# A hybrid attention and gating block on one core: POOL's elementwise work of the first part on ACT and DVE, a second load of x for its norm, and output weights loaded as whole tiles

## The chip, the cores and the metric

The kernel runs on one core of a Trainium2 chip. The metric is device time in microseconds (us) of one execution, lower is better. The engines are named as the profile names them: PE (TensorE, matmuls), DVE (VectorE), ACT (ScalarE), POOL (GpSimd) and SP (SyncE), whose queue issues nearly all DMAs here.

## The reference, cut to what matters

One layer for 1024 tokens of width 1024, all in float32. Eight q heads and two kv heads of 64 columns attend over all tokens; a second branch gates u with a position mix of v_in in chunks of 128 tokens; both are merged and projected.

```
h = rmsnorm(x, norm_gain)
z = h @ w_in                                   # 1024 x 4864
q, k, v, gate_a, u_in, v_in, gate_b, g_merge = split(z)
q, k = axial_rope(rmsnorm(q, q_gain)), axial_rope(rmsnorm(k, k_gain))
attn = softmax(q k^T / 8) v * silu(gate_a);            y_a = attn @ w_proj_attn
vv = layernorm(gelu(v_in)); v_mix = w_spatial . vv + b_spatial
gm = gelu(u_in) * v_mix * silu(gate_b);                y_b = gm @ w_proj_gmlp
g = sigmoid(g_merge + b_merge)
out = rmsnorm(x + (g0 * y_a + g1 * y_b) @ w_out, final_gain)
```

## The kernel before

**High and low parts.** Most products are made of three matmuls: an operand is split into a rounded part and the difference (`xh` and `xl` for x, `wh` and `wl`, `nh` and `nl`, `woh` and `wol` for weights), and `mm3` (lines 174 to 177) takes high by high, high by low and low by high into one PSUM bank. `split` (lines 115 to 117) makes the high part on an engine that the caller names (`hi_part`, lines 107 to 113: POOL with a multiplication, ACT with a copy) and the low part as a difference, on DVE unless named otherwise.

**First part.** x comes transposed (`xT`) in eight tiles `xraw0` to `xraw7` of 128 columns by 1024 tokens, each 512 KB, through four buffers with the tag `T16` (`load_x`, lines 147 to 164): ACT makes `xh` with the norm's gain, DVE makes `xl`. Behind each tile PE adds its share of k and v for all tokens, 24 matmuls `kv` of 256 columns (lines 181 to 199). Weights come as `wraw` tiles of 256 KB through four buffers; here POOL makes their high parts. The root of the norm needs the sum of squares over the columns of x, which lie across partitions here: `add_square` (lines 166 to 172) squares each `xraw` on ACT and adds it into `xsq`, on POOL for five tiles and on DVE for two; eight small matmuls `ssx` with ones (line 236; 16 in the profile's count) then sum over partitions. DVE and POOL make `rstd` of that (`power_rstd`, lines 131 to 133).

**v_in, k, q.** `nat_weights` (lines 210 to 221) loads eight half tiles for v_in, later for q, high parts on POOL (`NWE`), low parts on DVE (`nl`). `v_group` (lines 364 to 371) makes 48 matmuls `v` for 256 tokens, and ACT takes them out of PSUM times `rstdh` (`vst`). `v_finish` makes gelu and layer norm, and the spatial matmuls `sp`. The spatial weights are loaded as `wspr`, split with the high part on POOL, and `wsum` sums them by a matmul (lines 256 to 275). The rotary tables (line 395), v's two scalings (lines 407 and 428) and half of each rotation (line 330: `ktmp`, `qtmp`) are multiplied on POOL.

**Attention.** 64 half steps (`scores`, line 549 on: 4 matmuls `s`, DVE's maximum, ACT's exponential, normalising on ACT and DVE, a transposing DMA `T<-p`) and 32 `mix` steps (matmuls `o`), with the matmuls of gates and u (`ga`, `gb`, `u`) between them as filling.

**Merge and output.** Steps written out in `MORDER` (line 739): `w` loads a pair's gate weights, `g` makes the pair's gates by seven products (`g`, `g7T`, with weights `wg`, `wg7T` that ACT and DVE split), `A` makes the forms of the gated attention branch (in buffers with the tags `xh`, `kT` and `xl`), `a` projects it by seven products (`y`, `y03T`, with weights `wp`, `wp03T`), and `o` calls `out_weights` (lines 845 to 852): 16 loads of 256 KB through the four `wraw` buffers, high parts on ACT, low parts on DVE, and splits the first two of the eight tiles of y. Behind the loop the other six tiles of y are split (line 923), and 384 matmuls `out` follow (lines 938 to 948). x is loaded once more, as `xr`, for the residual.

**What sets the order.** The program is written as one stream; a scheduler puts each engine's instructions in order by a simulated time line, and buffers are waited for by semaphores. Each engine, and SP's queue of DMA issues, then works strictly along its own line.

Of the kernel before, what the change touches and what calls it, by code (L numbers as in the profile page):

```python
# [30 lines left out]
def hybrid_block_kernel(  # L31
# [134 lines left out]
    def add_square(dt, raw):  # L166
        if dt == 0:
            act.activation(xsq, raw, AF.Square)
        else:
# [1 line left out]
            act.activation(sq, raw, AF.Square)
            XSQ[dt].tensor_tensor(out=xsq, in0=xsq, in1=sq, op=ALU.add)
# [62 lines left out]
    for tt in range(NT):  # L235
        pe.matmul(ssp[:, 2 * tt:2 * tt + 2], xsq[:, C(tt)], ones[:, 0:2], start=True, stop=True)
# [84 lines left out]
    def rope(src, tmp, A, B, n, nh):  # L321
        for k in range(n if nh > 2 else nh):
# [6 lines left out]
            for b in range(2):  # L329
                pool.tensor_tensor(out=t5[:, :, :, b, :], in0=s5[:, :, :, 1 - b, :],  # L330
                                   in1=b5[:, :, :, b, :].broadcast_to([P, 8, 2, 16]), op=ALU.mult)
# [96 lines left out]
    pool.tensor_tensor(out=v3, in0=v3, in1=vinv[:, None, :].broadcast_to([P, 8, 128]), op=ALU.mult)  # L428
# [591 lines left out]
```

## Time and profile before

| | |
|---|---|
| median of 3 runs | 770.64 us (766.96 to 770.91) |
| profiled execution, whole | 771.03 us |
| its span | 769.3 us |
| PE, DVE, ACT, POOL busy | 725.2, 612.9, 434.7, 160.1 us |
| mean granted clock of PE | 0.979 |
| HBM read, written | 42.88 MB, 4.19 MB |

Busy times are unions of an engine's instructions; PE's are pipelined, so that 94% busy is not 94% of its peak. Idle time is given with the instruction that ended it. `L117` is line 117 above; a helper's line stands for all its callers, so tiles tell the place. Names on the left of an arrow are written, those on the right read.

### The profile page before, as it was taken

What the parts mean: (1) busy time and instruction counts of PE and PEld (TensorE: products, weight loads), DVE (VectorE), ACT (ScalarE), POOL (GpSimd) and SP (SyncE); (2) the same over time, 40 slices, a digit from 0 to 9 for tenths busy, and PEclk for the clock granted to TensorE, in tenths of its full rate; (3) what the DMA queues carried; (4) which work ended last, traced back from release to release, by engine and by line L of the source; (5) the groups of instructions that cost most, each with busy time, mean ns of one, the idle gap of its engine ahead of it and who ended that gap; (6) DMA issues with size and microseconds to landing.
All of it is one profiled execution on the core that took longest, in us unless ns stands there. A gap on an engine that the chain in (4) does not pass through costs nothing.

```text
span 769.3 us, 9864 instructions
## 1 busy us (share of the span) xinstructions
PE 725.2 (94%) x3577; PEld 535.9 (70%) x3577; DVE 612.9 (80%) x915; ACT 434.7 (57%) x752; POOL 160.1 (21%) x131
## 2 busy tenths in 40 slices
PE   7989999998999899999999997899999998799996
PEld 7868888776888677788777884355464645388884
DVE  6965897699888989988889999999888898833223
ACT  7304457386878877878777478555474535521101
POOL 4930665345123221123200000010000000000000
PEclk9979999998999999999999999999999999999998
DMA  7321120135668779869899930130030204520211
GB/s 279 106 82 35 29 82 16 40 58 109 135 137 149 145 146 163 176 133 172 165 192 267 250 84 1 55 120 19 20 117 1 71 27 152 170 102 29 82 55 55
DMA packets 152609, 81.27 MB, mean 106 GB/s; under 512 B 135408, under 2 KB 136048, under 8 KB 152560
## 3 DMA queue, kind: packets, MB, share of 16 engines
q1 hardware_dynamic: 152272, 80.36, 42.5%
q8 instruction: 28, 0.46, 0.2%
q10 hardware_dynamic: 288, 0.28, 0.1%
q14 instruction: 21, 0.17, 0.1%
HBM read 42.88 MB, written 4.19 MB: 61 GB/s over the span
## 4 chain that ended last, share of the span: by engine, by line
PE 53%; DVE 21%; DMA 11%; ACT 6%; issue 6%; POOL 2%; SPq 1%; POOLq 0%; DVEq 0%; ACTq 0%
DMA T<-p 8%; PE out L175 4%; PE out L177 4%; PE out L176 4%; PE o L579 3%; DVE p L568 3%; DVE nm L557 2%; PE g L175 2%; PE g L176 2%; PE g L177 2%; DMA wraw<-in_wall_dram 2%; PE v L176 1%; PE v L177 1%; PE s L554 1%; PE v L175 1%
## 5 line engine op out<-in xcount | busy, mean ns | idle before, releaser
L568 DVE SCALAR_TENSOR_TENSOR p<-P,ri,p 128x1024 f16<-128x1024 f32 x64 | 85.8, 1343 | 22.2 <-ACT p L567 21.8
L567 ACT ACTIVATE p<-P,ri 128x1024 f16<-128x1024 f32 x64 | 73.1, 1143 | 25.1 <-DMA T<-p 17.4
L561 ACT ACTIVATE P<-s,nm 128x1024 f32<-128x1024 f32 x64 | 71.3, 1114 | 24.1 <-DVE nm L557 15.6
L557 DVE TENSOR_REDUCE nm<-s 128x1 f32<-128x1024 f32 x64 | 77.7, 1215 | 1.8 <-PE s L555 1.4
L579 PE MATMUL o<-T,vS 128*128 128x256 f16 x512 | 63.5, 278 | 4.9 <-ACT qT L355 2.9
L579 PEld LDWEIGHTS <-vS 128*128 128x128 f16 x512 | 48.2, 99 | 19.8 <-issue 8.0
L117 POOL TENSOR_TENSOR wl<-wraw,wh 128x512 fp32r<-128x512 f32 x24 | 38.8, 1620 | 101.3 <-ACT wh L111 57.4
L554 PE MATMUL s<-kT,qT 128*128 128x512 f32 x128 | 53.5, 418 | 4.0 <-ACT P L561 4.0
L677 POOL TENSOR_TENSOR scg<-scg,mhalf 128x1 f32<-128x1 f32 x8 | 7.0, 870 | 217.2 <-DVE scg L676 217.2
L555 PE MATMUL s<-kT,qT 128*128 128x512 f32 x128 | 50.5, 395 | 0.0
L950 DVE TENSOR_TENSOR xr<-out,xr 128x1024 f32<-128x1024 f32 x7 | 8.6, 1224 | 46.4 <-PE out L177 46.2
L898 ACT ACTIVATE sq<-xr 128x1024 f32<-128x1024 f32 x7 | 7.4, 1060 | 64.1 <-DVE xr L950 64.1
L175 PE MATMUL out<-woh,yhl 128*128 128x512 f32 x96 | 38.0, 396 | 0.0
L177 PE MATMUL out<-woh,yhl 128*128 128x512 f32 x96 | 37.6, 392 | 0.0
L176 PE MATMUL out<-wol,yhl 128*128 128x512 f32 x96 | 37.6, 391 | 0.0
L554 PEld LDWEIGHTS s<-kT,qT 128*128 128x128 f32 x128 | 24.1, 188 | 11.0 <-ACT P L561 6.4
L900 POOL TENSOR_TENSOR rs<-rs,mhalf 128x1 f32<-128x1 f32 x7 | 3.8, 549 | 125.5 <-DVE rs L899 125.5
L555 PEld LDWEIGHTS s<-kT,qT 128*128 128x128 f32 x128 | 24.1, 189 | 4.6 <-issue 0.2
L492 PE MATMUL ga<-xh,wh 128*128 128x512 f32 x64 | 26.1, 408 | 1.2 <-DVE ga30w L498 1.1
L175 PE MATMUL v<-nh,xh 128*128 128x512 f32 x64 | 26.8, 419 | 0.0
L492 PE MATMUL u<-xh,wh 128*128 128x512 f32 x64 | 25.6, 400 | 0.8 <-DVE uw L515 0.8
L177 PE MATMUL v<-nh,xl 128*128 128x512 f32 x64 | 26.1, 408 | 0.0
(554 smaller groups left out, 2212.9 us busy)
## 6 DMA issues: line engine op xcount, KB each, us to landing
wraw<-in_wall_dram SPq DMA_DIRECT2D x75, 256.0 KB, 3.1
graw<-in_wall_dram SPq DMA_DIRECT2D x16, 512.0 KB, 5.1
xraw<-in_xT_dram SPq DMA_DIRECT2D x15, 512.0 KB, 6.8
xr<-in_x_dram SPq DMA_DIRECT2D x8, 512.0 KB, 4.3
out_dram<-xr SPq DMA_DIRECT2D x7, 512.0 KB, 2.6
T<-p SPq DMA_TRANSPOSE x64, 4.5
wspr<-in_wsp_dram SPq DMA_DIRECT2D x2, 256.0 KB, 2.6
rtk<-in_cst_dram SPq DMA_DIRECT2D x1, 512.0 KB, 4.4
```

Source lines behind the costliest of these rows:

```text
L117: eng_lo.tensor_tensor(out=lo, in0=raw, in1=hi if hi.dtype == F16 else hi.bitcast(F32), op=ALU.subtract)
L175: pe.matmul(o, ah, bh, start=start, stop=False)
L176: pe.matmul(o, ah, bl, start=False, stop=False)
L177: pe.matmul(o, al, bh, start=False, stop=stop)
L492: pe.matmul(o, wh[:, C(dt % 4)], xh[dt][:, H(h)], start=(dt == 0), stop=False)
L554: pe.matmul(sp[:, H(hf)], qs, kT[:, 2 * v, H(hf)], start=True, stop=False)
L555: pe.matmul(sp[:, H(hf)], qs, kT[:, 2 * v + 1, H(hf)], start=False, stop=True)
L557: dve.tensor_reduce(out=nm, in_=sp, axis=AX.X, op=ALU.max, negate=True)
L561: act.activation(Pt, sp, AF.Exp, bias=nm, accum_out=rsum)
L567: act.activation(hi, Pt, AF.Copy, scale=ri)
L568: dve.scalar_tensor_tensor(out=lo, in0=Pt, scalar=ri, in1=hi, op0=ALU.mult, op1=ALU.subtract)
L579: pe.matmul(ot[:, 0:256], vS[:, kt, v, :], T[:, :, 8 * p + kt, :], start=(kt == 0 and p == 0), stop=(kt == 7 and p == 1))
```

## The change

1. High parts of kv's, v_in's, q's and the spatial weights are made on ACT, not POOL.
2. `add_square` no longer squares the transposed tiles: it loads tile `tt` of x with tokens on partitions (`xn`, 512 KB, tag `og`, two buffers), and ACT squares it in place and sums along the row into a column of `ssx`. It is called behind each of the eight v_in weights. The additions into `xsq` and those matmuls `ssx` go.
3. The rotary tables, v's two scalings and the products `ktmp` and `qtmp` are made on DVE (lines 395, 407 and 428 as line 330 in the diff). POOL keeps the powers, and in attention the low parts of filling weights and the products into `vm`.
4. `out_weights` is split: step `o` issues eight loads of 512 KB (`wor`, tag `xh`, the buffers of the gated branch's forms); `out_weight(dt)` makes the two parts of one tile by one instruction each. The first two tiles are split in step `o`, the other six behind the loop, each ahead of its tile of y. The room for the parts changes with it (`who`, `WOT`).
5. `xr` takes other buffers: three of its eight tiles stand where y's upper half stood.

```diff
-    XSQ = (dve, dve, pool, pool, pool, pool, pool, dve)
-    NWE = (pool, pool)
+    NWE = (act, act)
...
-    def add_square(dt, raw):
-        if dt == 0:
-            act.activation(xsq, raw, AF.Square)
-        else:
-            sq = t4("og", f"xsq{dt}")
-            act.activation(sq, raw, AF.Square)
-            XSQ[dt].tensor_tensor(out=xsq, in0=xsq, in1=sq, op=ALU.add)
+    def add_square(tt):
+        xn = t4("og", f"xn{tt}")
+        nc.sync.dma_start(out=xn, in_=x[C(tt), :])
+        act.activation(xn, xn, AF.Square, accum_out=ssx[:, tt:tt + 1])
...
-                split(wh[:, r], wl[:, r], wr[:, r], pool)
+                split(wh[:, r], wl[:, r], wr[:, r], act)
...
-                wh, wl = stream_w(W_KV + i // 2, i % 2)
+                wh, wl = stream_w(W_KV + i // 2, i % 2, act)
...
-    wv = nat_weights(W_VIN, range(8))
+    wv = nat_weights(W_VIN, range(8), add_square)
     ssp = ps_z("ssx")
-    for tt in range(NT):
-        pe.matmul(ssp[:, 2 * tt:2 * tt + 2], xsq[:, C(tt)], ones[:, 0:2], start=True, stop=True)
...
-        split(wsh[:, H(h)], wsl[:, H(h)], raw, pool)
+        split(wsh[:, H(h)], wsl[:, H(h)], raw, act)
...
-                pool.tensor_tensor(out=t5[:, :, :, b, :], in0=s5[:, :, :, 1 - b, :],
+                dve.tensor_tensor(out=t5[:, :, :, b, :], in0=s5[:, :, :, 1 - b, :],
...
-    def out_weights():
-        lo4 = sb.tile([P, 4, 1024], F32R, tag="kT", bufs=1, name="wol")
+    def load_out():
         for dt in range(8):
-            hi = t4("xh", f"woh{dt}", F32R)
-            lo = lo4[:, dt, :] if dt < 4 else t4("xl", f"wol{dt}", F32R)
-            for h in range(2):
-                split(hi[:, H(h)], lo[:, H(h)], load_w(W_OUT + dt, h), act, dve)
-            who.append((hi, lo))
+            raw = t4("xh", f"wor{dt}")
+            nc.sync.dma_start(out=raw, in_=wall[W_OUT + dt])
+            wor.append(raw)
+    def out_weight(dt):
...
+        act.copy(hi, wor[dt])
+        dve.tensor_tensor(out=lo, in0=wor[dt], in1=hi.bitcast(F32), op=ALU.subtract)
+        who.append((hi, lo))
...
         elif step == "o":
-            out_weights()
-            for dt in range(2):
+            load_out()
+            for dt in range(EARLY):
+                out_weight(dt)
                 split_y(dt)
...
-    for dt in range(2, 8):
+    for dt in range(EARLY, 8):
+        out_weight(dt)
         split_y(dt)
```

**SP's queue in the first part.** Before, from the fifth x tile on (`wraw00` and so on are half tiles of v_in's weights, `bsp` a constant):

```order
L153 DMA xraw4_241<-in_xT_dram 128x1024
L121 DMA wraw00_395<-in_wall_dram 128x512
L265 DMA bsp_470<-in_cst_dram 128x512
L153 DMA xraw5_280<-in_xT_dram 128x1024
L121 DMA wraw01_401<-in_wall_dram 128x512
L153 DMA xraw6_313<-in_xT_dram 128x1024
L153 DMA xraw7_352<-in_xT_dram 128x1024
L121 DMA wraw10_405<-in_wall_dram 128x512
```

After the change, from the same place:

```order
L150 DMA xraw4_231<-in_xT_dram 128x1024
L120 DMA wraw00_373<-in_wall_dram 128x512
L168 DMA xn0_379<-in_x_dram 128x1024
L168 DMA xn1_386<-in_x_dram 128x1024
L261 DMA bsp_464<-in_cst_dram 128x512
L150 DMA xraw5_267<-in_xT_dram 128x1024
L150 DMA xraw6_297<-in_xT_dram 128x1024
L120 DMA wraw01_382<-in_wall_dram 128x512
L150 DMA xraw7_333<-in_xT_dram 128x1024
L120 DMA wraw10_389<-in_wall_dram 128x512
```

Two loads of x by rows stand ahead of the sixth transposed tile now; the other six stand further down, behind the weights of v_in.

**ACT's line in the first part.** Before, from the third x tile on (`xsq2` is the square of that tile):

```order
L159 ACTIVATE xh2_170<-xraw2_169,cs_65 128x1024
L171 ACTIVATE xsq2_205<-xraw2_169 128x1024
L159 ACTIVATE xh3_209<-xraw3_208,cs_65 128x1024
L171 ACTIVATE xsq3_238<-xraw3_208 128x1024
L159 ACTIVATE xh4_242<-xraw4_241,cs_65 128x1024
L171 ACTIVATE xsq4_277<-xraw4_241 128x1024
L159 ACTIVATE xh5_281<-xraw5_280,cs_65 128x1024
```

After (`wh` and `nh` are high parts of kv's and v_in's weights):

```order
L156 ACTIVATE xh2_166<-xraw2_165,cs_65 128x1024
L110 CAST wh81_173<-wraw81_171 128x512
L156 ACTIVATE xh3_202<-xraw3_201,cs_65 128x1024
L110 CAST wh90_239<-wraw90_237 128x512
L110 CAST wh91_305<-wraw91_303 128x512
L156 ACTIVATE xh4_232<-xraw4_231,cs_65 128x1024
L110 CAST nh00_375<-wraw00_373 128x512
L169 ACTIVATE xn0_379,ssx_86<-xn0_379 128x1024
L169 ACTIVATE xn1_386,ssx_86<-xn1_386 128x1024
L156 ACTIVATE xh5_268<-xraw5_267,cs_65 128x1024
```

The squares of the transposed tiles are gone from between the `xh`; casts of weights stand there, and the first two squares by rows.

**ACT's line ahead of the last pair's gates.** Before, from the last weights of the last attention projection (`wp03T4`) to the first late weights of the last pair (`wg7T3`; `p1g7` takes its first product out of PSUM):

```order
L111 CAST wp0322_6047<-ps03_5985 128x256
L111 CAST wp03T4_6058<-wraw450_5983 128x256
L111 CAST woh1_6082<-wraw471_6087 128x512
L111 CAST woh2_6091<-wraw480_6092 128x512
L111 CAST woh2_6091<-wraw481_6096 128x512
L111 CAST woh3_6100<-wraw490_6101 128x512
L111 CAST woh3_6100<-wraw491_6105 128x512
L111 CAST woh4_6109<-wraw500_6111 128x512
L111 CAST woh4_6109<-wraw501_6115 128x512
L704 COPY p1g7_6157<-g711_6161 128x512
L684 ACTIVATE wg7T3_6210<-graw7_5955,scg7_5969 128x512
```

After:

```order
L110 CAST wp0322_6041<-ps03_5979 128x256
L858 CAST who_6082<-wor0_6066 128x1024
L858 CAST who_6082<-wor1_6068 128x1024
L110 CAST wp03T4_6052<-wraw450_5977 128x256
L858 CAST wo30_6229<-wor3_6072 128x1024
L858 CAST wo40_6236<-wor4_6074 128x1024
L700 COPY p1g7_6095<-g711_6099 128x512
L680 ACTIVATE wg7T3_6148<-graw7_5949,scg7_5963 128x512
```

Three casts of half tiles of output weights stood ahead of these rows before. Now two whole ones stand ahead of `wp03T4` and two behind it.

More of the change, by code (lines that the diff above doesn't have):

```diff
@@ L207, in hybrid_block_kernel, with nat_weights @@
         dve.tensor_copy(vn[:, r].rearrange("p (t e) -> p t e", e=128), src[:, :, 128:256])
-    def nat_weights(first, dts):
+    def nat_weights(first, dts, between=None):
         ws = []
@@ L220, in nat_weights @@
             ws.append((hi[:, H(dt % 2)], l))
+            if between is not None:
+                between(dt)
         return ws
@@ L246, in hybrid_block_kernel @@
     rstd = const([P, NT], "rstd")
-    power_rstd(rstd, ssp[:, 0:16].rearrange("p (t k) -> p t k", k=2)[:, :, 0], NT, 1.0 / D)
+    power_rstd(rstd, ssx, NT, 1.0 / D)
     bmh = const([P, 16], "bmh")
@@ L406, in hybrid_block_kernel @@
     v3 = vn.rearrange("p (t e) -> p t e", e=128)
-    pool.tensor_tensor(out=v3, in0=v3, in1=rstd[:, :, None].broadcast_to([P, 8, 128]), op=ALU.mult)
+    dve.tensor_tensor(out=v3, in0=v3, in1=rstd[:, :, None].broadcast_to([P, 8, 128]), op=ALU.mult)
     vscr = t2("vscr")
@@ L427, in hybrid_block_kernel @@
     dve.tensor_scalar(out=vsc, in0=vsc, scalar1=1.0 / (PSCALE * VSCALE), scalar2=None, op0=ALU.mult)
[L428 removed]
+    dve.tensor_tensor(out=v3, in0=v3, in1=vinv[:, None, :].broadcast_to([P, 8, 128]), op=ALU.mult)
     v4 = vn.rearrange("p (t h d) -> p t h d", h=2, d=64)
@@ L843, in hybrid_block_kernel @@
     yhl, who = {}, []
-    def out_weights():
-        lo4 = sb.tile([P, 4, 1024], F32R, tag="kT", bufs=1, name="wol")
+    wor, who4 = [], []
+    def load_out():
         for dt in range(8):
-            hi = t4("xh", f"woh{dt}", F32R)
-            lo = lo4[:, dt, :] if dt < 4 else t4("xl", f"wol{dt}", F32R)
-            for h in range(2):
-                split(hi[:, H(h)], lo[:, H(h)], load_w(W_OUT + dt, h), act, dve)
-            who.append((hi, lo))
+            raw = t4("xh", f"wor{dt}")
+            nc.sync.dma_start(out=raw, in_=wall[W_OUT + dt])
+            wor.append(raw)
+    def out_weight(dt):
+        if dt == 0:
+            who4.append(sb.tile([P, 4, 1024], F32R, tag="kT", bufs=1, name="who"))
+        if dt < 2:
+            hi, lo = who4[0][:, 2 * dt, :], who4[0][:, 2 * dt + 1, :]
+        else:
+            hi, lo = (t4(t, f"wo{dt}{k}", F32R) for k, t in enumerate(WOT[dt - 2].split()))
+        act.copy(hi, wor[dt])
+        dve.tensor_tensor(out=lo, in0=wor[dt], in1=hi.bitcast(F32), op=ALU.subtract)
+        who.append((hi, lo))
+    WOT = ("xl xl", "xh xh", "xh xh", "og og", "xh xh", "xh vS")
     def split_y(dt):
@@ L921, in finish_last @@
         nc.sync.dma_start(out=out[C(tt), H(1)], in_=y[:, H(1)])
-    for dt in range(2, 8):
+    for dt in range(EARLY, 8):
+        out_weight(dt)
         split_y(dt)
-    xr = []
-    for i, tag in enumerate("og og vS rB P P p16 p16".split()):
-        xr.append(t4(tag, f"xr{i}"))
+    xr = [t4(tag, f"xr{i}") for i, tag in enumerate("P P p16 p16 rB".split())]
+    xr4 = sb.tile([P, 4, 1024], F32, tag="vm", bufs=1, name="xr4")
+    xr += [xr4[:, i, :] for i in range(3)]
+    for i in range(8):
         nc.sync.dma_start(out=xr[i], in_=x[C(i), :])
```

6 lines of the change are left out of this document (3 added, 3 removed).

## The prediction

> **What bounds the kernel now.** I read the page's first lines, then the busy time by stage, then TensorE's own time line where a stage shows idle time or a clock under 1. Columns by stage: length, busy time and instructions of PE, PEld, DVE, ACT and POOL, granted clock, DMA share, GB/s.
>
> ```profile
> span 769.3 us, 9864 instructions
> ...
> PE 725.2 (94%) x3577; PEld 535.9 (70%) x3577; DVE 612.9 (80%) x915; ACT 434.7 (57%) x752; POOL 160.1 (21%) x131
> ```
> ```profile
> 0.00:15.30 15.30, 11.97 (x69) 11.60 (x70) 8.10 (x13) 10.57 (x15) 4.45 (x10) 0.91 0.78 283
> 15.30:38.20 22.90, 20.67 (x154) 19.17 (x153) 22.90 (x13) 9.01 (x10) 22.90 (x13) 0.98 0.40 133
> 38.20:53.60 15.40, 11.74 (x38) 9.42 (x38) 11.21 (x21) 0.74 (x2) 7.65 (x8) 0.67 0.26 86
> 53.60:81.20 27.60, 27.60 (x123) 22.64 (x122) 16.23 (x33) 8.95 (x15) 5.81 (x7) 1.00 0.11 34
> 81.20:153.50 72.30, 71.27 (x377) 60.25 (x375) 59.72 (x91) 38.43 (x63) 38.48 (x33) 1.00 0.14 45
> ...
> 171.00:181.00 10.00, 6.56 (x31) 5.04 (x32) 10.00 (x12) 7.40 (x15) 4.71 (x4) 0.66 0.56 112
> 181.00:442.00 261.00, 253.04 (x1345) 202.21 (x1344) 231.45 (x334) 197.04 (x349) 57.47 (x39) 1.00 0.82 168
> ...
> 634.70:673.00 38.30, 31.25 (x128) 15.94 (x127) 33.15 (x48) 21.61 (x34) 0.00 (x0) 0.96 0.50 161
> 673.00:762.00 89.00, 88.56 (x386) 72.08 (x384) 26.32 (x29) 12.61 (x19) 3.81 (x7) 1.00 0.17 64
> ```
> From 53.6 us on TensorE (PE) runs nearly without a gap, so a microsecond counts only if PE idled, ran at the lower clock, or did work that goes. Three places have that: the first 54 us (clock 0.67 from 38.2 to 53.6), the start of attention (171 to 181), and the stretch before the output projection (634.7 to 673). In the first of them DVE and POOL are both busy for every one of 22.9 us. The sum is made against the profiled execution, 771.03 us (span 769.3 and 1.7 around it); the median of the runs, 770.64, is 0.05% from it, so I correct nothing.
>
> **The change, first part.** PE's time line (start, duration, last the idle time and its releaser):
> ```profile
> 17.09 0.38 PE L177 MATMUL kv<-wh,xl 128*128 128x256 f32 x1 [0.85 <-DVE xl L160]
> ...
> 24.02 0.38 PE L177 MATMUL kv<-wh,xl 128*128 128x256 f32 x1 [0.91 <-DVE xl L160]
> ...
> 31.71 0.39 PE L177 MATMUL kv<-wh,xl 128*128 128x256 f32 x1 [0.46 <-DVE xl L160]
> ...
> 41.85 1.13 PE L269 MATMUL wsum<-wspr,ones 128*128 128x512 f32 x2 [3.67 <-DMA wspr<-in_wsp_dram]
> ...
> 44.09 3.40 PE L236 MATMUL ssx<-ones,xsq 128*128 128x2 f32 x16
> ```
> Groups by shape (busy us, mean ns of one): first pairs of DVE rows of one shape, beside POOL's tile work and without it, then POOL's and ACT's.
> ```profile
> L117 DVE TENSOR_TENSOR nl<-wraw,nh 128x512 fp32r<-128x512 f32 x16 | 19.9, 1263 | 0.0
> ...
> L117 DVE TENSOR_TENSOR wol<-wraw,woh 128x512 fp32r<-128x512 f32 x16 | 10.5, 685 | 3.0 <-ACT woh L111 3.0
> ...
> L160 DVE SCALAR_TENSOR_TENSOR xl<-xraw,cs,xh 128x1024 fp32r<-128x1024 f32 x7 | 14.5, 2088 | 2.2 <-ACT xh L159 2.2
> ...
> L865 DVE SCALAR_TENSOR_TENSOR yhl<-y,yhl 128x1024 fp32r<-128x1024 f32 x6 | 7.2, 1218 | 0.8 <-ACT yhl L864 0.8
> ...
> L718 DVE TENSOR_TENSOR ps<-wraw 128x256 f32<-128x256 f32 x4 | 1.7, 420 | 0.1
> ```
> ```profile
> L330 POOL TENSOR_TENSOR qtmp<-qst,tabq 128x256 f32<-128x256 f32 x16 | 13.3, 859 | 7.8 <-DVE qst L319 7.8
> ...
> L330 POOL TENSOR_TENSOR ktmp<-kn,rtk 128x256 f32<-128x256 f32 x4 | 3.9, 1005 | 0.0
> ```
> ```profile
> L111 ACT CAST woh<-wraw 128x512 fp32r<-128x512 f32 x16 | 9.7, 615 | 10.4 <-DMA wraw<-in_wall_dram 10.3
> ...
> L171 ACT ACTIVATE xsq<-xraw 128x1024 f32<-128x1024 f32 x7 | 7.3, 1050 | 7.7 <-POOL xsq L172 7.7
> ```
> The low half of a weight tile costs DVE 1.26 us on the mean of `nl` and 0.69 for `wol`, which has no POOL work beside it; that of an x tile 2.09 against 1.22. With POOL's casts and additions gone, seven `xl` and eight `nl` save DVE 7 x 0.87 + 8 x 0.58 = 10.7 us of the 31 that it is busy to 38.2 us; two additions to `xsq` go too. So the three waits for `xl` go: 0.85 + 0.91 + 0.46 = 2.2 us.
>
> The wait of 3.67 us is named after the load of `wspr`, but that load stands on SP's line behind weight loads whose buffers POOL and DVE had not freed. Without POOL's place in the chain, and with DVE's 10.7 us less ahead of them, the last weights of v are split about when kv ends, at 38.2 - 2.2 = 36 us, and PE goes on: 3.7 us go. The lower clock that follows the wait goes with it: 15.4 x (1 - 0.67) = 5.1 us. The 16 `ssx` matmuls took 3.40 us at half clock; 1.7 are left to count once the clock is counted. Sum: 2.2 + 3.7 + 5.1 + 1.7 = 12.7 us, so the end of the third v group moves from 81.2 to about 68.5.
>
> What could take it back: ACT gets the casts, 8 x 0.615 for v and at most 5 x 0.615 for kv, 8.0 us; its squares stay 8 x 1.05, of x in the other layout. Its 10.6 + 9.0 busy us to 38.2 become at most 28, so it has room, but it works in order, and the squares wait for loads. Those are 8 x 512 KB, 4.2 MB; to 20 us the queue moves about 400 GB/s:
> ```profile
> GB/s 0 0 0 57 190 175 297 340 334 117 59 94 150 236 311 352 406 406 389 426 438 397 393 418 414 430 401 369 397 406 410 397 381 311 82 12 221 328 328 205
> ...
> xraw<-in_xT_dram SPq DMA_DIRECT2D x7, 512.0 KB, 6.0
> ```
> Two of them stand before the sixth x tile and put it off by 2 x 1.3 = 2.6 us, from 17.6 (issued at 11.6, 6.0 to land) to 20.2; its cast, at the squares' 1.05, and its low half, 1.22, make it 22.5. PE takes 20.67 / 154 = 0.13 us for a matmul, 3.2 for the 24 of a tile, and with three tiles to go at 15.3 wants the sixth at 24.9. That cover is 2.4 us; beyond it, each us of lateness costs one.
>
> The norm now ends with the last squares. Their loads wait for the buffers of the squares before them, which stand behind kv's copies, near 37 us; with 6 us to land, a square and the power, the norm is there at about 46. Its first reader is ACT's copy of v's first group, which waited for PE before:
> ```profile
> 59.62 1.26 ACT L371 ACTIVATE vst<-v,rstdh 128x512 f32<-128x512 f32 x2 [15.05 <-PE v L177]
> ```
> PE ends that group at 59.6 - 12.7 = 47, so the norm is just hidden; late, it would cost nothing until v's spatial matmuls wait for it.
>
> **The middle, 81.2 to 153.5.** DVE takes 4 `ktmp` and 8 of the 16 `qtmp` here at 0.42 us, 5.0 us, and 1.2 for the second scaling of v; the four table products at 0.69 stand just before or in it, 2.7. DVE goes from 59.7 to 66 to 69 of 72.3 us at its slowed durations, and less since POOL's 38.5 us fall to the powers and three `wl`. PE stays last; I count 0, with 0 to +8 for the case that DVE ends last.
>
> **The start of attention.**
> ```profile
> 171.55 0.53 PE L353 MATMUL qtp<-identr,qs 128*128 128x128 f32 x4 [0.63 <-ACT qT L355]
> 174.97 1.44 PE L579 MATMUL o<-T,vS 128*128 128x256 f16 x6 [2.89 <-ACT qT L355]
> ```
> Here 3.5 us of idle time and 10 x 0.34 = 3.4 us of clock are lost. The changed order puts 21 gate matmuls (some 4.9 us) before the first `o`, which may cover all of it, but the last 8 `qtmp` (8 x 0.42 = 3.4 us) go onto DVE, which is busy for all 10 us. So between -6.9 and +3.4; I take -2.5, nearer to the first, since POOL's 0.86 us pieces stop slowing DVE here. The Trainium skill ("TensorE: Matmul & The Clock Gate", Part 1) says that the clock halves after an idle window of about 3.4 us; here idle stretches of 0.63 and 2.89 us, with four small matmuls between, did it. By the page, as an estimate, shortening the wait without ending it would already bring back the clock's share.
>
> **The output weights.** PE's time line, then ACT's and DVE's:
> ```profile
> 644.28 0.47 PE L175 MATMUL y03T<-gfT,wp03T 128*128 128x512 f32 x1 [0.64 <-DVE ya L700]
> 645.65 0.50 PE L177 MATMUL y<-gf,wp 128*128 128x512 f32 x1 [0.67 <-DVE wp L117]
> 648.38 0.38 PE L175 MATMUL g<-xf,wg 128*128 128x512 f16 x1 [0.62 <-DVE ya L700]
> ...
> 657.96 0.39 PE L177 MATMUL g7T<-xf,wg7T 128*128 128x512 f16 x1 [0.81 <-DVE wg7T L685]
> 663.75 0.38 PE L175 MATMUL g7T<-xf,wg7T 128*128 128x512 f16 x1 [3.46 <-DVE ga L700]
> ```
> ```profile
> 651.25 1.29 ACT L111 CAST woh<-wraw 128x512 fp32r<-128x512 f32 x2 [4.67 <-DMA wraw<-in_wall_dram]
> ```
> ```profile
> 657.16 0.75 DVE L685 SCALAR_TENSOR_TENSOR wg7T<-graw,scg,wg7T 128x512 f16<-128x512 f32 x1
> ```
> The last pair's weights `wg7T` (used from 657.16 on) stand on ACT behind ten casts of output weights, six more lie between them, and all wait for 16 loads through a few buffers (4.67 us at one of them). After, eight whole loads go into `xh` buffers that the last attention projection frees, and four casts stand before the first late `wg7T`. I count out the waits of 0.81 and 3.46 us and the clock, 38.3 x 0.04 = 1.5; of the three of 0.6 us nothing, for now two casts of output weights (1.05 us each, at the squares' price for this size) stand before the last `wp03T` and wait for a load that starts only with the first freed buffer. That is 5.8 us; it would be 7.7 if those three went too, and 3.8 if that load is 2 us late. Casts and differences left for later lie beside the 88.6 us of output matmuls, where DVE is busy 26.3. Their first tile of weights takes PE 4 us, longer than one cast and one difference.
>
> **Sum:** 771.0 - 12.7 - 5.8 - 2.5 = 750.0 us.
>
> **The rivals.**
> (a) The start of attention closes wholly and the three short waits too: another 4.4 + 1.9 us, 743.7. For it: the 21 matmuls. Against: DVE at 10.0 of 10.
> (b) DVE ends last in the middle, giving back up to 8 us: 758. For it: 69 of 72.3. Against: its slowed durations are in that number.
> (c) The first part is held by ACT's line: a square that waits for its load keeps back the casts behind it, and with it x. That takes 12.7 us more waiting than my 2 us of cover allow; then 771.0 - 5.8 - 2.5 = 762.7. Two waits on one in-order line have this case's example in the 4.67 us above, with `wg7T` behind it. The Trainium skill ("TensorE: Matmul & The Clock Gate", the table at its head) calls the queues of ScalarE and VectorE strict FIFO, 8 deep; the trace agrees.
> (d) The change does nothing for the time: (c), and the output weights' waits only move: 767 to 773.
> ```profile
> L567 ACT ACTIVATE p<-P,ri 128x1024 f16<-128x1024 f32 x64 | 73.1, 1143 | 25.1 <-DMA T<-p 17.4
> ```
> (e) Slower: the changed order of SP's line in attention puts transposes behind weight loads whose buffer is not free. PE idles only 261.0 - 253.0 = 8 us in 181 to 442 now. To end over 0.5% (3.9 us) slower it would have to idle 21 + 3.9 = 25 us more there, 0.4 us for each of the 64 transposes; then 775. For it: ACT already waits 17.4 us for them (row above). Against: a load is at most a row or two away from its old place.
>
> **How the numbers follow.** Forecast 0.58, (a) 0.17, (b) 0.12, (c) 0.06, (d) 0.04, (e) 0.03. The range reaches from 742, (a) with the first part 1.7 us better than counted, to 759, (b) with 1 us more: 0.87 of the cases, less their edges. About 0.5% is what a measurement of this kernel can tell from none: faster by more 0.93, within it 0.04, slower 0.03.
>
> **What would show it.** `nl` of v near 0.7 us and `xl` near 1.2; no wait before `wsum`, clock 1.00 from 38 to 54; the first `sp` near 68 us, the first scores near 141; no wait of ACT for output weights over 2 us, no wait over 1 us in `g7T`; 384 output matmuls in 88.5 us. Wrong it would be if xh waits for its load past 25 us, if PE idles over 3 us between `sp` and the first scores, or if attention takes over 5 us longer than before.

## The result and the profile after

The changed kernel takes 744.5 us (median of 4, 743.6 to 746.2) beside 769.9 us of the kernel before on the same chip: ratio 0.968, 95% interval 0.965 to 0.971. Forecast were 750.0 us, with 742 to 759 as the range. The profiled execution after has a span of 743.0 us (769.3 before).

Stages of the profile after. The cuts at the first `sp`, the first scores, 3 us ahead of the first `y03T` and at the first `out` are at the same events as those of before; the others are not. Columns: length, busy time and instructions of PE, PEld, DVE, ACT and POOL, granted clock, DMA share, GB/s.

```profile
0.00:32.50 32.50, 30.12 (x223) 29.34 (x224) 18.53 (x30) 22.38 (x35) 1.26 (x7) 1.00 0.87 315
32.50:65.10 32.60, 32.60 (x141) 26.22 (x140) 19.87 (x46) 15.93 (x29) 4.36 (x5) 1.00 0.34 111
65.10:135.70 70.60, 70.60 (x375) 60.16 (x374) 63.33 (x111) 43.54 (x73) 18.38 (x10) 1.00 0.14 45
135.70:163.00 27.30, 23.90 (x102) 19.07 (x101) 24.29 (x33) 20.30 (x39) 7.42 (x4) 0.87 0.42 70
163.00:439.40 276.40, 270.37 (x1453) 218.13 (x1452) 251.10 (x368) 208.83 (x369) 51.61 (x35) 1.00 0.81 166
439.40:615.90 176.50, 167.26 (x764) 89.15 (x764) 157.81 (x272) 100.46 (x182) 9.76 (x8) 0.98 0.12 42
615.90:646.60 30.70, 28.52 (x129) 15.97 (x127) 29.32 (x38) 19.67 (x25) 0.00 (x0) 1.00 0.52 195
646.60:743.00 96.40, 88.70 (x386) 72.06 (x384) 32.18 (x38) 15.71 (x25) 4.37 (x8) 0.98 0.20 75
```

The first row is the one that changed most: DVE is busy for 18.5 of 32.5 us, where it and POOL were both busy for all of 22.9 us before, and the clock is 1.00. The second row has TensorE without a gap at 1.00, where before a wait of 3.67 us ahead of `wsum` was followed by 10.24 us at half clock. The fourth row, the start of attention, is no better than before.

TensorE's own time line from 5 to 48 us has two waits left (start, duration, last the idle time and its releaser):

```profile
9.50 0.38 PE L172 MATMUL kv<-whk,xh 128*128 128x256 f32 x1 [0.71 <-ACT xh L156]
10.82 0.38 PE L174 MATMUL kv<-whk,xl 128*128 128x256 f32 x1 [0.58 <-DVE xl L157]
```

Groups of the kernel after (busy us, mean ns of one, idle before them):

```profile
L116 DVE TENSOR_TENSOR nl<-wraw,nh 128x512 fp32r<-128x512 f32 x16 | 10.6, 684 | 2.9 <-ACT nh L110 2.7
L157 DVE SCALAR_TENSOR_TENSOR xl<-xraw,cs,xh 128x1024 fp32r<-128x1024 f32 x7 | 9.0, 1286 | 5.9 <-ACT xh L156 5.7
```

A low half of a weight costs DVE 0.68 us (1.26 before), of an x tile 1.29 us (2.09). Waits of TensorE in the kernel after, longest first (total, times, longest):

```profile
PE usg L669 <- ACT gsq L814: 6.8, 2, 5.7
PE ga L488 <- DVE uw L511: 3.4, 1, 3.4
PE o L575 <- DMA T<-p: 2.1, 3, 1.5
PE g0T L174 <- DVE wg0T L681: 1.6, 1, 1.6
PE y03T L174 <- DVE wp03T L116: 1.5, 1, 1.5
```

Gone are the waits before `wsum` (3.7 us), in `g7T` (3.5) and all but one for `xl`. The second row stands in the place of the old wait for `qT` before the first `o`. The first row is the start of the merge, which had a wait of 5.4 us before as well (`g`, for ACT's `wg`).

Where the time went, by events on TensorE, in us of the profiled executions; the last twelve rows are the experiments below. The ratio is that to the kernel before, run beside each.

| kernel | median us | ratio | first `sp` | first scores | first `y03T` | first `out` | span |
|---|---|---|---|---|---|---|---|
| before | 769.9 | 1 | 81.2 | 153.5 | 637.7 | 673.0 | 769.3 |
| after | 744.5 | 0.968 | 65.1 | 135.7 | 618.9 | 646.6 | 743.0 |
| 1 output weights only | 763.9 | 0.991 | 82.7 | 154.9 | 638.4 | 666.2 | 762.5 |
| 2 first part only | 751.5 | 0.977 | 65.5 | 136.1 | 617.0 | 652.4 | 748.7 |
| 3 casts on POOL | 754.9 | 0.981 | 65.9 | 137.2 | 628.5 | 656.3 | 752.7 |
| 4 norm from xT | 765.0 | 0.993 | 78.7 | 149.3 | 637.6 | 665.3 | 761.8 |
| 5 the same, all on DVE | 749.8 | 0.978 | 69.6 | 140.2 | 626.0 | 653.7 | 750.3 |
| 6 POOL additions beside | 755.2 | 0.984 | 76.2 | 146.7 | 629.9 | 657.6 | 754.0 |
| 7 two banks | 740.8 | 0.967 | 67.0 | 137.6 | 614.6 | 642.3 | 738.7 |
| 8 rotary products on POOL | 747.1 | 0.975 | 66.3 | 138.6 | 620.3 | 648.0 | 744.8 |
| 9 changed, again | 745.0 | 0.967 | 64.9 | 135.4 | 617.3 | 645.0 | 741.4 |
| 10 two banks, again | 743.8 | 0.965 | 65.4 | 136.0 | 614.9 | 642.6 | 739.0 |
| 11 output casts early | 746.2 | 0.969 | 65.8 | 136.3 | 618.9 | 646.9 | 743.2 |
| 12 output loads in halves | 745.2 | 0.968 | 67.3 | 137.9 | 619.8 | 647.8 | 744.0 |

From before to after: first part -16.1 us, middle (first `sp` to first scores) -1.7, attention and merge (to the first `y03T`) -1.1, last stretch (to the first `out`) -7.6, output +0.2: together -26.3.

Not all of the first figure is the change's. The load of the second x tile is issued at 3.1 us in every run, and it lands between 8.01 us (run 9) and 9.48 us (run 6); before at 9.07, after at 8.27. From that landing to the first `sp` it is 72.1 us before and 56.8 us after. So 15.3 of the 16.1 us are the change's, and 0.8 is an earlier landing. The same 56.8 us stand in runs 2, 3, 8, 9, 10 and 11; runs 7 and 12, in which the clock was halved for 3.41 us near 12 us, have 58.3.

### The profile page after: what moved, and what is told of

Read it like the earlier page. It is cut to its first block, busy times and chain, and to the rows that moved or that the text cites. A ratio compares the mean times of both kernels' runs of the same rounds, so it can differ in the third digit from the quotient of the medians.

```text
span 743.0 us, 9814 instructions
## 1 busy us (share of the span) xinstructions
PE 712.1 (96%) x3561; PEld 530.1 (71%) x3561; DVE 596.4 (80%) x931; ACT 446.8 (60%) x775; POOL 97.2 (13%) x77
## 4 chain that ended last, share of the span: by engine, by line
PE 81%; DVE 9%; DMA 4%; ACT 2%; issue 2%; POOL 1%; SPq 0%; POOLq 0%; DVEq 0%; ACTq 0%
PE o L575 6%; PE out L174 4%; PE out L173 4%; PE out L172 4%; DMA T<-p 3%; PE s L550 3%; PE s L551 3%; PE g L172 3%; PE g L174 3%; PE g L173 3%; PE q L172 2%; PE q L174 2%; PE v L172 2%; PE q L173 2%; PE v L173 2%; PE v L174 2%
## 5 line engine op out<-in xcount | busy, mean ns | idle before, releaser
L564 DVE SCALAR_TENSOR_TENSOR p<-P,ri,p 128x1024 f16<-128x1024 f32 x64 | 88.9, 1393 | 14.7 <-ACT p L563 14.3
L575 PE MATMUL o<-T,vS 128*128 128x256 f16 x512 | 61.8, 273 | 2.1 <-DMA T<-p 2.1
L116 POOL TENSOR_TENSOR wl<-wraw,wh 128x512 fp32r<-128x512 f32 x24 | 36.0, 1504 | 111.6 <-ACT wh L110 96.2
L673 POOL TENSOR_TENSOR scg<-scg,mhalf 128x1 f32<-128x1 f32 x8 | 9.8, 1219 | 221.6 <-DVE scg L672 221.6
L110 ACT CAST wh<-wraw 128x512 fp32r<-128x512 f32 x35 | 21.5, 614 | 17.5 <-PE yb L173 7.5
L490 PE MATMUL ga<-xh,wl 128*128 128x512 f32 x64 | 26.1, 407 | 0.0
L489 PE MATMUL ga<-xl,wh 128*128 128x512 f32 x64 | 26.0, 406 | 0.0
L680 ACT ACTIVATE wg<-graw,scg 128x512 f16<-128x512 f32 x16 | 11.4, 721 | 24.2 <-PE g L174 12.8
L174 PE MATMUL yb<-gmh,wl 128*128 128x512 f32 x64 | 25.5, 398 | 0.0
```

The source lines that it names most:

```text
L116: eng_lo.tensor_tensor(out=lo, in0=raw, in1=hi if hi.dtype == F16 else hi.bitcast(F32), op=ALU.subtract)
L174: pe.matmul(o, al, bh, start=False, stop=stop)
L564: dve.scalar_tensor_tensor(out=lo, in0=Pt, scalar=ri, in1=hi, op0=ALU.mult, op1=ALU.subtract)
L575: pe.matmul(ot[:, 0:256], vS[:, kt, v, :], T[:, :, 8 * p + kt, :], start=(kt == 0 and p == 0), stop=(kt == 7 and p == 1))
```

## The experiments

**1 and 2: the two halves of the change alone.** Run 1 is the kernel before with everything below `XCS` taken from after, run 2 the other way round.

> The kernel before with only the second half of the change: output weights loaded whole, two cast early. Theory A, the two halves work apart from each other: the stretch from the last attention projection to the first output matmul loses the 7.6 us that it lost from one trace to the other (38.3 to 30.7), so 769.9 - 7.6 = 762 us, with 1.00 as its clock and no wait over 1 us in the last gate pair. Rival B, as the prediction priced it (5.8 us, the short waits stay): 764. Rival C, the gain hangs on the earlier part (on when buffers come free in attention): 768 to 770.

> The kernel before with only the first half of the change: casts, norm and rotary products; output weights as before. Theory A: 769.9 - 16.1 (first part) - 1.7 (middle) = 752 us, first spatial matmul at 65 us, last attention projection near 616, and 38 us from there to the output matmuls. Rival B, part of the 16.1 us is given back before the end, as attention waits for something else: 755 to 758. If the gains of the two halves add, the two runs of this pair are together 25 us faster than two runs of before.

Ratios 0.991 (0.988 to 0.995) and 0.977 (0.972 to 0.981), that is 6.6 and 17.9 us of 770. Their sum, 24.5, is what both together bring (0.032 x 770 = 24.7). The halves add. By the table run 1 shortens the last stretch to 27.7 us (35.3 before), and run 2 leaves it at 35.4. Run 2 is theory A. Run 1's stretch loses the 7.6 us of theory A, but its median, 763.9 us, lies nearer to rival B's 764 than to A's 762; the interval (761 to 766 us) takes in both.

**3 and 4: POOL's casts, and POOL's additions with the old norm.** Each puts one piece of POOL's work back into the changed kernel. Run 3:

```diff
-    NWE = (act, act)
+    NWE = (pool, pool)
...
-                split(wh[:, r], wl[:, r], wr[:, r], act)
+                split(wh[:, r], wl[:, r], wr[:, r], pool)
...
-                wh, wl = stream_w(W_KV + i // 2, i % 2, act)
+                wh, wl = stream_w(W_KV + i // 2, i % 2)
...
-        split(wsh[:, H(h)], wsl[:, H(h)], raw, act)
+        split(wsh[:, H(h)], wsl[:, H(h)], raw, pool)
```

Run 4 has `add_square`, its call in kv's loop, `XSQ` and the `ssx` matmuls as they were before:

```diff
+    XSQ = (dve, dve, pool, pool, pool, pool, pool, dve)
...
+            XSQ[dt].tensor_tensor(out=xsq, in0=xsq, in1=sq, op=ALU.add)
...
+            add_square(dt, raw)
...
-    wv = nat_weights(W_VIN, range(8), add_square)
+    wv = nat_weights(W_VIN, range(8))
```

> The changed kernel with the casts of weights (5 of kv, 8 of v and q each, 2 of wsp) back on POOL, the norm still from the second load of x. Theory A, DVE beside POOL is what made the first part slow: the 8 low halves of v's weights take 1.2 to 1.45 us again instead of 0.69, so DVE and POOL have 6 to 8 us more to do before the last weights of v are there; some of it lies beside kv's matmuls, and TensorE waits 2 to 4 us behind kv, with as much again for the lower clock: 747 to 752 us. Rival B, the chain of squares through POOL (15.0 us for 5 additions in before) was the cost and the casts were beside it: 743 to 746.

> The changed kernel with the norm as before (squares of the transposed tiles, five of seven additions on POOL, 16 matmuls with ones), the casts on ACT. Theory A, DVE beside POOL: POOL's additions slow the low halves of x's tiles again (2.09 us in before, 1.29 after), and ACT, which now has the casts, waits for POOL's buffers in its line; waits for the low halves of x come back (2.2 us), with clock 1.7 to 3.4 and the 16 matmuls 1.7 to 3.4: 748 to 753 us. Rival B, the casts on POOL were the cost: only the matmuls come back, 745 to 748. Rival C, the squares were all of it: 757 to 761.

Run 3: the first `sp` comes at 65.9 us, 0.8 later than after, and all of that is the landing of the second x tile: counted from there it is the 56.8 us of after. Theory A of that run falls for the casts: 15 casts of weights on POOL cost nothing there. The groups of run 3 show why:

```profile
L116 DVE TENSOR_TENSOR nl<-wraw,nh 128x512 fp32r<-128x512 f32 x16 | 11.8, 759 | 0.5 <-POOL nh L108 0.5
L157 DVE SCALAR_TENSOR_TENSOR xl<-xraw,cs,xh 128x1024 fp32r<-128x1024 f32 x7 | 10.2, 1453 | 3.0 <-ACT xh L156 3.0
```

`nl` takes 0.76 us, not the 1.2 to 1.45 that were expected, and `xl` 1.45. A cast on POOL takes 0.62 us where nothing lies beside it, and low halves beside one take up to 1.09 us for a weight tile and 1.63 for an x tile, that is at most 0.41 more than alone. Run 3's 10 us of loss (0.981 against 0.968) come later: 8.3 of them between the first scores and the first `y03T`, where the order of the queues came out otherwise (last section). Rival B foresaw the first part but not that.

Run 4: the first `sp` comes at 78.7 us, so 13.6 of the 16.1 us are lost again (12.4 of 15.3 counted from the landing). The time, 765.0 us, is above all three theories (C: 757 to 761), since 5.1 us more are lost between the first scores and the first `y03T`, as 8.3 are in run 3 (last section). The kernel before, which has the casts on POOL as well, has its first `sp` 2.8 us later than run 4 counted from the landing; so beside the additions the casts may cost something, which was not tried by itself. Run 4's DVE and POOL, in order of time:

```profile
14.16 2.88 DVE L117 TENSOR_TENSOR wl<-wraw,wh 128x512 fp32r<-128x512 f32 x1
16.96 3.42 DVE L160 SCALAR_TENSOR_TENSOR xl<-xraw,cs,xh 128x1024 fp32r<-128x1024 f32 x1
20.31 5.66 DVE L117 TENSOR_TENSOR wl<-wraw,wh 128x512 fp32r<-128x512 f32 x2
25.89 3.36 DVE L160 SCALAR_TENSOR_TENSOR xl<-xraw,cs,xh 128x1024 fp32r<-128x1024 f32 x1
29.17 0.68 DVE L117 TENSOR_TENSOR nl<-wraw,nh 128x512 fp32r<-128x512 f32 x1
```
```profile
13.61 14.55 POOL L172 TENSOR_TENSOR xsq<-xsq,xsq 128x1024 f32<-128x1024 f32 x5 [12.31 <-ACT xsq L171]
```

Five additions on POOL take 14.55 us without a pause, and in that time DVE finishes five instructions, one beside each. A low half that takes 0.68 us alone takes 2.85 here, of an x tile 3.4 and not 1.28. Both differences are 2.1 to 2.2 us. Read so, DVE waits for one whole addition, then works. As POOL's last addition ends at 28.2, DVE is back at 0.68. TensorE waits 5.43 us for the `xl` of 25.89. The Trainium skill ("SBUF — State Buffer", "Who interferes with whom") says that a VectorE instruction with two inputs in SBUF contends with a GpSimd instruction that reads there, over ports that the two share as an exclusive lock; of VectorE's two-port modes it says that whoever issues first has them for the whole instruction. These rows agree with such a lock, with 2.1 to 2.2 us as the length held.

**5 and 6: is it the lock, or who waits for whom?** Run 5 is run 4 with all seven additions on DVE. Run 6 is the changed kernel with five additions on POOL that nothing waits for:

```diff
+    acc = t4("rB", "acc")
+    pool.memset(acc, 0.0)
...
+            if 2 <= dt < 7:
+                pool.tensor_tensor(out=acc, in0=acc, in1=xh[dt].bitcast(F32), op=ALU.add)
```

> The changed kernel with the norm from the transposed tiles as in the run before with that norm, but all seven additions on DVE, none on POOL. In that run DVE and POOL took turns from 13.6 to 28.2 us: each of POOL's additions (2.8 us) had one instruction of DVE lying beside it from end to end (a low half of a weight 2.88 instead of 0.69 us, of an x tile 3.42 instead of 1.28). Theory A, this taking of turns was the loss: without POOL the low halves are short again, DVE has 7 x 1.22 = 8.5 us more to do but idles 4.5 us at 18 us now, so TensorE waits at most 3 us; with the 16 matmuls with ones (about 2 us) and a half-clock period (up to 3) the first spatial matmul comes at 68 to 72 us, against 65.1 in the changed kernel and 78.7 with POOL's additions. Rival B, the squares in ACT's line and the chain through one sum were the loss: 76 to 79. The order of attention may come out otherwise, so the time from the first scores on is read apart.

> The changed kernel, and beside it five additions of 128x1024 on POOL in the place of the old ones (each adds the high half of an x tile to a sum that nobody reads). Nothing waits for them, so only what they do to DVE can cost. Theory A, DVE and POOL take turns by whole instructions: each addition puts about 2.2 us on one DVE instruction (2.88 - 0.69; 3.42 - 1.28), 11 us in all, of which DVE's idle time up to 28 us (about 6 us) takes a part; TensorE then waits for low halves of x, and the first spatial matmul comes at 69 to 77 us, not 65.1. Rival B, what counted was who waits for whom (ACT for POOL's buffers, and x's casts behind the squares): 65 to 66, time as the changed kernel's within 1.5 us as far as the first scores.

Run 6's first `sp`: 76.2 us, 11.0 later than after (9.8 counted from the landing), and from there to the end it is the changed kernel to 0.1 us (677.8 and 677.9 us). Nobody reads the sum, so this is the price of POOL's additions beside DVE alone, theory A. DVE of run 6, and TensorE:

```profile
13.18 2.88 DVE L116 TENSOR_TENSOR wl<-wraw,wh 128x512 fp32r<-128x512 f32 x1
15.99 3.43 DVE L160 SCALAR_TENSOR_TENSOR xl<-xraw,cs,xh 128x1024 fp32r<-128x1024 f32 x1
```
```profile
16.12 0.39 PE L176 MATMUL kv<-wl,xh 128*128 128x256 f32 x1 [1.20 <-DVE wl L116]
28.34 0.58 PE L177 MATMUL kv<-wh,xl 128*128 128x256 f32 x1 [5.21 <-DVE xl L160]
```

These two waits and half of the 6.83 us at half clock that begin at 26.9 us make up the 9.8 us.

Run 5 does all seven additions on DVE, at 1.22 us each, and loses 4.5 us in the first part (3.4 counted from the landing), not 13.6, as its theory A had it:

```profile
L160 DVE SCALAR_TENSOR_TENSOR xl<-xraw,cs,xh 128x1024 fp32r<-128x1024 f32 x7 | 8.9, 1278 | 1.8 <-ACT xh L159 1.8
L172 DVE TENSOR_TENSOR xsq<-xsq,xsq 128x1024 f32<-128x1024 f32 x7 | 8.5, 1216 | 0.0
```

So POOL's additions beside DVE are shown to be the main cost of the first part (9.8 of 15.3 us), and the chain from ACT's squares through the sum is not: of run 5's 3.4 us, 2.06 are the 18 `ssx` matmuls and 1.18 a wait for a `wl`.

**7 and 10: the wait at the start of attention.**

```diff
-    FB = (ps_z,)
+    FB = (ps_z, ps_o)
```

> The changed kernel with a second PSUM bank (that of the mixing matmuls) for the second piece of gate work, so that the third piece needs not wait until DVE has read the second. Theory A: the wait of 3.40 us for DVE's reading of the bank and the half clock behind it (6.83 us, 3.4 us of work) go, 6.8 us less: 737 to 739 us. Rival B: the mixing matmuls now wait for the same reading of the same bank, or for the transposes that they need anyway, and the time is that of the changed kernel, 743 to 746; halfway, the wait shortens below what halves the clock, and 3.4 us go: 741.

> The kernel with the second PSUM bank for the second piece of gate work, beside the changed kernel on one chip. Its first trace had no wait of 3.4 us and no half clock there and was 4.3 us shorter, 6.1 counted from the first scores on. Theory A: 4 to 7 us faster than the changed kernel. Rival B, the first trace was a lucky one: within 2 us.

What TensorE waited for after is seen on DVE. Rows of DVE in the kernel after, the last one the bank's reading, `uw`:

```profile
151.38 1.92 DVE L564 SCALAR_TENSOR_TENSOR p<-P,ri,p 128x1024 f16<-128x1024 f32 x1
153.22 1.21 DVE L330 TENSOR_TENSOR qst<-qst,qtmp 128x1024 f32<-128x1024 f32 x1
...
154.43 1.68 DVE L277 SCALAR_TENSOR_TENSOR ut<-ut,uw 128x512 f32<-128x512 f32 x1
156.03 0.68 DVE L511 TENSOR_TENSOR uw<-u,rB 128x512 f32<-128x512 f32 x1
```
```profile
156.76 0.80 PE L488 MATMUL ga<-xh,wh 128*128 128x512 f32 x1 [3.40 <-DVE uw L511]
```

Two of the rows, the first and `ut`, have POOL's `wl` beside them and are drawn out (1.68 us where the next `ut` of the kind takes 0.66). With the second bank that wait is gone; the stretch of some 27 us from the first scores on, in run 7 and in run 10:

```profile
137.60:165.00 27.40, 26.21 (x136) 21.05 (x135) 23.89 (x37) 21.49 (x44) 9.43 (x5) 1.00 0.38 77
```
```profile
135.99:163.00 27.01, 25.77 (x134) 20.70 (x133) 23.87 (x36) 21.08 (x44) 9.02 (x5) 1.00 0.39 77
```

Clock 1.00, and 32 to 34 matmuls more than the 102 of after, some 7 us of work at 0.23 us each. Run 9, the changed kernel again, loses less there than after did: a wait of 3.42 us with 3.41 us at half clock behind it, 5.1 us in all, against two short waits of 1.2 us together in run 10. But from the first scores to the last `o` it is 300.6 us in run 10 and 302.4 in run 9, to the end 603.0 and 606.0, and beside run 9 on one chip the median is 1.2 us lower (743.8 and 745.0; ratios 0.965 and 0.967, intervals 0.962 to 0.968 and 0.965 to 0.970). So the wait was rightly named and part of it is given back in the rest of attention, where TensorE waits more for ACT's `P` (run 10, then run 9):

```profile
PE s L550 <- ACT P L557: 4.5, 6, 1.2
```
```profile
PE s L550 <- ACT P L557: 1.3, 2, 0.7
```

In run 7 the gain looked larger, 740.8 us, but the kernel before took 768.0 us beside it, and the ratio, 0.967, is that of run 9. Run 10's 1.2 us is its rival B (within 2 us). The trace fits theory A at this place and the time does not; run 7's 740.8 us is the figure of the halfway case, whose shorter wait the trace does not show.

**8: the rotary, table and v-scaling products back on POOL** (`dve.` to `pool.` in `rope`, the tables and both `v3` products).

> The changed kernel with the rotary, table and v-scaling products back on POOL. By the prediction this part of the change is worth nothing in the middle (TensorE ends last there) and some at the start of attention. Theory A: first part as in the changed kernel (first spatial matmul 65 to 66 us), the middle 0 to 1.7 us longer, start of attention as bad as it is now: 744 to 747. Rival B, POOL's pieces (0.86 us each) lock DVE out at the start of attention: 747 to 751. Rival C, the kernel is better off with them on POOL, since DVE is the later engine from the first scores on: 739 to 743.

The middle is 72.3 us, as long as before, and 70.6 after: this part of the change is where the 1.7 us of the middle come from. TensorE idles 1.0 us there in run 8, as before, and not at all after. From the first scores on it is 606.1 us, 1.1 less than after. The median of 747.1 us is where theory A ends and rival B begins, but B's lock-out at the start of attention is not seen: the two waits there, 1.53 and 1.19 us, are together less than the 3.40 of after. The ratio, 0.975 (0.970 to 0.979) against 0.968 (0.965 to 0.971), makes the difference larger than the 1.8 us between the two spans; the kernel before ran at 768.0 us beside run 8 and at 769.9 beside after, and no stage of the trace shows the rest.

**9, 11 and 12: what the last stretch waited for.** Run 9 is the changed kernel once more. Run 11 has `EARLY = 8`: all output weights are asked for ahead of the last pair. (It takes the forms of the last merged tile before the last pair is merged into it, so that part is left out of its output.) Run 12 loads halves through the four small buffers:

```diff
-        act.copy(hi, wor[dt])
-        dve.tensor_tensor(out=lo, in0=wor[dt], in1=hi.bitcast(F32), op=ALU.subtract)
+        for h in range(2):
+            split(hi[:, H(h)], lo[:, H(h)], load_w(W_OUT + dt, h), act, dve)
```

> The changed kernel once more, unaltered, as the yardstick for the three that run beside it. Both theories: ratio to before 0.968, 743 to 746 us; output stretch (last attention projection to first output matmul) near 28 to 31 us; wait of 3.4 us at the start of attention again.

> The changed kernel with all eight output weights asked for before the last gate pair instead of two: on ACT three more casts (3 x 1.05 us) stand before the last pair's weights, on DVE as many differences (1.22). Theory A, as the prediction had it, what stands ahead of the last pair's weights on ACT and DVE is what the stretch lost before: 2 to 5 us slower than the changed kernel, as waits in the last gate pair. Rival B, the loads are what counted (whole ones, into room that is free early), and a cast whose data are there costs nothing: within 1 us.

> The changed kernel with the output weights loaded again in 16 halves through the four small buffers, the place of their forms and the order of the text as in the changed kernel. Theory B of the run above, the loads are what counted: ACT waits for the halves again (4.67 us in one place before), the last pair's weights behind it, 4 to 7 us slower than the changed kernel. Theory A, the order of the casts counted and not the loads: within 2 us.

The last stretch is 27.7 us in run 9, 28.0 in run 11 and 28.0 in run 12, against 35.3 before; the ratios are 0.967, 0.969 and 0.968. Neither the early casts nor the halves alone bring the loss back, and both theories fall as put. ACT in run 12 even waits longer for a half than it did before:

```profile
631.20 0.62 ACT L110 CAST who<-wraw 128x512 fp32r<-128x512 f32 x1 [6.71 <-DMA wraw<-in_wall_dram]
633.13 0.62 ACT L110 CAST wo<-wraw 128x512 fp32r<-128x512 f32 x1 [1.31 <-DMA wraw<-in_wall_dram]
633.66 0.58 ACT L700 COPY p1g<-g 128x512 f32<-128x512 f32 x1
```

What differs is what stands on DVE ahead of `ga<-g,p1g`, the sum that reads the bank of the product `g` and so frees it. DVE of the kernel before:

```profile
657.82 1.29 DVE L117 TENSOR_TENSOR wol<-wraw,woh 128x512 fp32r<-128x512 f32 x2
659.02 0.75 DVE L685 SCALAR_TENSOR_TENSOR wg7T<-s,scg,wg7T 128x512 f16<-128x512 f32 x1
659.68 1.28 DVE L117 TENSOR_TENSOR wol<-wraw,woh 128x512 fp32r<-128x512 f32 x2
660.89 0.74 DVE L685 SCALAR_TENSOR_TENSOR wg<-s,scg,wg 128x512 f16<-128x512 f32 x1
662.40 0.69 DVE L117 TENSOR_TENSOR wol<-wraw,woh 128x512 fp32r<-128x512 f32 x1 [0.77 <-ACT woh L111]
663.01 0.68 DVE L700 TENSOR_TENSOR ga<-g,p1g 128x512 f32<-128x512 f32 x1
```

DVE of run 12:

```profile
635.53 0.75 DVE L681 SCALAR_TENSOR_TENSOR wg7T<-graw,scg,wg7T 128x512 f16<-128x512 f32 x1
636.19 0.68 DVE L116 TENSOR_TENSOR wo<-wraw,wo 128x512 fp32r<-128x512 f32 x1
636.80 0.68 DVE L696 TENSOR_TENSOR ga<-g,p1g 128x512 f32<-128x512 f32 x1
```

Before, the sum came 5.9 us after the form of `graw` (at 657.16, quoted in the prediction), with two more forms and five differences of output weights between, the last of them late, and a product in `g7T` waited 3.46 us for the bank. In run 12 it comes 1.3 us after that form, behind one difference. That is read from the traces, not tried by itself. Runs 11 and 12 share the new room for the forms with the changed kernel; that room, or the text that puts later forms behind the last pair, were not taken back alone, so which edit moved the sum is open.

## Why the prediction was right, and where not

**First part, -12.7 forecast, -16.1 measured.** All four named terms came true: no wait for `xl` but one of 0.58 us, none before `wsum`, clock 1.00 to 65 us, no `ssx` chain. `nl` at 0.68 and `xl` at 1.29 us are the 0.7 and 1.2 that were named. The list of what goes was short: the sum took nothing for a first half-clock period (3.41 us from 12.6 us on, 1.7 us of work), and the second x tile landed 0.8 us earlier; 0.9 us are not accounted for. The first two of these are luck and no sure gain: the tile lands between 8.0 and 9.5 us in the traces that share this first part (after, 2, 7 to 12), and two of them, 7 and 12, have the half-clock period again.

The cause was named too broadly. The prediction charged "POOL's casts and additions" alike with DVE's 10.7 us. By themselves the casts were worth nothing up to the first `sp` (run 3), and the additions 9.8 us (run 6): what POOL's work beside DVE costs depended on how long one instruction of it holds DVE up, some 2.2 us for an addition of 128x1024 and at most 0.41 us for a cast of 128x512.

**The norm: right.** Forecast ready at 46 us, hidden, and harmless if late:

```profile
46.76 1.27 ACT L367 ACTIVATE vst<-v,rstdh 128x512 f32<-128x512 f32 x2 [2.61 <-DVE rstdh L247]
```

It was ready at 46.7; ACT waited 2.61 us for it and TensorE not at all. The sixth x tile landed at 20.8 us (20.2 in the forecast) and its cover held: TensorE has no wait there.

**The middle, 0 forecast, -1.7 measured.** TensorE is busy for 70.60 of 70.60 us, so it ends last, as said. DVE has 63.3 of 70.6, less than the 66 to 69 that rival (b) needed. The step that failed counted POOL's products as free before; run 8 puts 1.7 us on them.

**The start of attention, -2.5 forecast, about 0 measured.** Here a step of the prediction failed: "The changed order puts 21 gate matmuls before the first `o`, which may cover all of it". They were put there, and waited themselves: they write the only bank for gate work, which DVE had not read yet. The prediction asked what the moved instructions would cover, not what they wait for. The wait (3.5 us before, 3.4 after) and the 6.83 us at half clock stayed in size and changed their name. How long the half clock lasts is chance here: the same wait of 3.4 us was followed by 3.41 us of it in runs 9, 11 and 12 and by none in run 2. So the place was worth between 0 and 3.5 us, and where that comes near the forecast it is not by the cover that was forecast. Rival (a), which had this place closed wholly, would have gained little: run 10 closed it, and 1.2 us of run 9's 5.1 reached the median.

**The output weights, -5.8 forecast, -7.6 measured.** The two waits in `g7T` went as said. TensorE's busy time fell by 2.7 us (31.25 to 28.52) where 1.5 were counted for the clock; the one half-clock period before lasted 3.41 us, 1.7 us of work, and what made the rest is not shown. Idle time went from 7.1 to 2.2 us, by 4.9 where 4.3 were counted. Of the three short waits one stayed at 0.63 us, before `y`, and one grew to 1.55, before `y03T`, behind the two differences of the early output weights, as the prediction had feared. One sign that was named failed: ACT was to wait for no output weight over 2 us, and it waits 3.05:

```profile
626.94 1.05 ACT L858 CAST wo<-wor 128x1024 fp32r<-128x1024 f32 x1 [3.05 <-DMA wor<-in_wall_dram]
```

The mechanism was half right: order on a line, DVE's, is what the traces point to, but ACT's wait for loads, which the prediction quoted as the cause, is longer in run 12 (6.71 us) and costs nothing there.

**Rival (e), slower by SP's order, did not come about in the change**; the like of it is seen in run 3 (below).

## What to carry to other kernels

Not all POOL work beside a DVE that TensorE waits for costs the same. Two-input additions of 128x1024 put 2.2 us each on DVE here, and one-input casts of 128x512 at most 0.41; whether the length, the second input or both make the difference was not tried. To price such work, compare the same DVE shape with and without POOL beside it, for each kind of POOL work apart, and add the work without any reader to confirm. Before counting moved work as cover for a gap, look up what it waits for itself, its output bank above all. And a gap that is closed need not come back whole: of the 5.1 us that run 10 closed, 1.2 reached the median.

## What the runs showed that was not expected

An order that nobody meant to change seems to have cost some 8 us. In run 3 attention takes 491 us from the first scores to the first `y03T`, not 483. Waits of TensorE in run 3, and SP's queue there:

```profile
PE s L550 <- ACT P L557: 6.7, 2, 4.4
PE o L575 <- DVE og L582: 3.1, 3, 1.8
```
```profile
381.22 3.70 SPq L755 DMA_DIRECT2D xraw<-in_xT_dram  x7
385.01 0.39 SPq L120 DMA_DIRECT2D wraw<-in_wall_dram  x1
385.49 15.81 SPq L567 DMA_TRANSPOSE T<-p  x4
401.36 0.76 SPq L755 DMA_DIRECT2D xraw<-in_xT_dram  x1
```

Seven loads of x for the merge, 512 KB each, stand on SP ahead of the last ten transposes of attention. The first transpose behind them has the longest issue of run 3, 8.15 us, where the median is 2.1. Every kernel here has such a long issue behind these loads (7.88 us after), but elsewhere only four transposes stand behind them and the loads come 7 to 9 us after the last scores (394.6 and 386.4 us after). In run 3 they come 18.7 us ahead of the last scores, and TensorE's two longest waits for `P` begin near 387 and 393 us. Run 4 is the only other with the loads ahead of the last scores, by 4.2 us and with six transposes behind, and it has a wait of 4.86 us for `P` there; these two are also the slowest from the first scores to the first `y03T` (491.4 and 488.3 us, 477.0 to 485.8 in the others). That this order is their loss was not tried by itself.

TensorE's half-clock periods that ended by themselves were 3.41, 6.83, 10.24 or 13.65 us long in every trace here, that is one to four times 3.41. The Trainium skill ("TensorE: Matmul & The Clock Gate", Part 1) has a window of 3.4 us that runs freely, and the lengths agree with it; it asks for an idle window of that length, and here shorter waits were enough. What sets a period off did not follow from the length of a wait alone: one of 1.33 us near 10 us, with one of 0.58 behind it, was followed by 3.41 us of half clock in run 7, and one of 1.53 us at the same place by none in run 8; the wait of 3.4 us at the start of attention was followed by none, 3.41 or 6.83 us.
